# Hybrid shortconv–SSD trunk, one core: the output projection's second quarter as seven block products, the scan split 20 + 12, the scan's norms in column groups

## The chip, the cores and the metric

One core of one Trainium2 chip runs the whole kernel in one launch. The metric is the device time in microseconds. The kernel before takes 2596.71 us (median of three runs, 2595.24 to 2597.68).

## The reference, cut to what matters

A layer of a hybrid encoder over 2048 positions of width 1024, in float32:

```python
h = rmsnorm(x, norm_mix_w)
u_b, u_c, u_h, z, xbc, dt_raw = split(h @ w_in)
y_a = u_b * causal_conv3(u_c * u_h)                      # 1024 columns
y_b = ssd_mixer(z, xbc, dt_raw, ...)                     # 1024 columns
x = x + concat([y_a, y_b]) @ w_out                       # 2048 x 1024
h = rmsnorm(x, norm_mlp_w)
x = x + square(relu(h @ w_up)) @ w_down
return rmsnorm(x, final_norm_w)
```

The SSD mixer runs a causal convolution and SiLU on `xbc`, then a chunked state-space scan over 16 heads in two groups, a skip term, a gate `silu(z)`, and an RMSNorm over each group's 512 columns with a gain:

```python
gated = (y * silu(z)).reshape(b, t, 2, 512)
gated = rmsnorm(gated, norm_w.reshape(2, 512))
```

The output projection therefore falls into quarters: half `i` of its input columns (0: the short convolution's y_a, 1: the scan's y_b) for half `h` of the positions (1024 each).

## The kernel before, in words

Everything lives transposed, with columns on the 128 partitions and positions along the free axis, in blocks of 512 positions (`b` = 0 to 3, `NB`); a half `h` is two such blocks. Each float32 operand of a large product is split into a rounded part `hi` (a ScalarE copy) and a rest `lo` (a VectorE subtraction), and a product is three 128x128 by 128x512 matmuls: hi·hi, hi·lo, lo·hi (`mm3`, lines 118 to 120, or the lines 315 to 317 inside `chain`).

**Seven block products.** A pair of output column tiles for one half of the positions is a 2x2 block product (two halves of the contraction, two position blocks). `Seven.chain` does it by seven block products instead of eight, in the order b11, t1, t2, b21, t3, b22, t4; one product is four tiles of the contraction, so 12 matmuls, and a pair is 84 matmuls where plain work needs 96. The activations have to stand as seven combinations per tile (three double tiles and one single, `places`), made once and spilled to DRAM as `..._d[h][k]`; the weights of a pair are combined on the way in (`combine`: four more VectorE additions on 512 columns, and four splits). The first product's sum is copied by ScalarE into the bank of the fourth (line 322). After each product `chain` calls `evict`, takes split weights of the next pair (`ahead`), and calls `after(name)`: one step.

**Refresh.** A change of half needs new places: `fetch` (line 379) loads four double tiles at a time and `settle` (lines 390, 391) splits them, spread over the steps of the pair ahead by `refresh`.

**Order of the stages.** First half of the input projection (20 pairs, `PAIRS`); second half (22 pairs, `LATER`, with z-, x-, ch- and b-pairs); the output projection; then the MLP, which also goes by seven products. `Proj.pair` evicts each pair; for a b-pair (y_a) of half 0 it stores the seven combinations in `ym_d`, for half 1 the four plain blocks in `ys_d`.

**The output projection** (`Output`). Quarter (0, half 0) is four pairs by seven products (`Output.pair`, 28 steps). The other three quarters are plain: `Output.unit`, one output tile for one position block, 24 matmuls; units 16 to 31 are quarter (0, half 1), 32 to 47 quarter (1, half 0), 48 to 63 quarter (1, half 1). `fill` splits a plain input for them; `schedule` lists at which hook each input is loaded and split.

**The scan** (`Scan`) is 32 chunks (4 position blocks, 2 groups, 4 chunks of 128 positions), a generator that is advanced one stage at a time from the steps and hooks of the product work. Chunks 0 to 15 run beside the second half's pairs, one stage per step, with single buffers (`bufs` = 1, nine stages per chunk); what is left is drained when the last pair but one begins. Chunks 16 to 31 run beside the output projection, double buffered, eight stages per chunk. In a chunk, `front` transposes the inputs (`ptx`, line 1417), copies them (`xtok`, 1422), multiplies them by decays (1432), splits (1438, 1440) and prepares the decay matrix `dec` (1437, 1439, 1445); `back` does the state matmuls (`st`, lines 118 to 120), the off-diagonal (`yo`, 1459) and diagonal products (`yd`, 1462), updates the state and gates the result. After the fourth chunk of a group, the square sums of its 512 columns go through `Rstd.parts` (hi and lo of a 128x512 tile) and `Rstd.whole` (two 128x512 matmuls with ones, lines 186 and 187, a square root and a 512-wide reciprocal, 188 and 189); for half 0 the result is stored (`rn_d`) and loaded again by `norm`, for half 1 it stays.

PSUM has eight banks: three turn for the products x and y (`mm`), one for w (`mw`), one each for `yo` and `yd`, and two for small things (`tp`). SyncE issues nearly all transfers, in one queue. The order of instructions on each engine is that of the program, as far as the planner of the tile framework does not pass one that is not ready.

Of the kernel before, what the change touches and what calls it, by code (L numbers as in the profile page):

```python
# [16 lines left out]
P = 128  # L17
# [23 lines left out]
def trunk(ctx: ExitStack, tc: tile.TileContext, x, w_in, w_dt, w_out, w_up, w_down, cvec, hrow, out):  # L41
# [19 lines left out]
    ym_d = [dram.tile([P, 7, TB], F32, name=f"ym_d{k}") for k in range(4)]  # L61
    wide = lambda n, k: [dram.tile([P, k, TH], F32, name=f"{n}_d{h}") for h in range(2)]
    xs_d, sz_d, ys_d, yn_d = wide("xs", 12), wide("sz", 8), wide("ys", 8), wide("yn", 8)
    rn_d = dram.tile([P, NBB, G, TB], F32, name="rn_d")
# [151 lines left out]
    class Seven:  # L216
# [156 lines left out]
        def fetch(self, h, i):  # L373
# [91 lines left out]
        def refresh(self, name):  # L465
# [5 lines left out]
            if i is not None:  # L471
                self.got = self.fetch(1, i)

    class Proj(Seven):
# [5 lines left out]
        LATER = "z0 x0 z4 ch0 ch4 b0 x8 ch1 ch5 b1 x2 ch2 ch6 b2 x4 x10 ch3 ch7 b3 x6 z6 z2".split()  # L480
# [296 lines left out]
        def pair(self, h, what, ws, ahead, after):  # L777
# [31 lines left out]
            def evict(name, gi, pm):  # L809
# [19 lines left out]
                elif name == "b22":  # L829
# [4 lines left out]
                    elif kind == "b":  # L834
                        mul(to["c12"], to["c12"], self.cc[n][:, hi])
                        if h:
                            nc.sync.dma_start(ys_d[h][:, n], a)
                        else:
                            e = s["e"] = self.wide("et")
                            self.sub(e[:, 0], a[:, hi], a[:, lo])  # L840
                            self.sub(e[:, 1], b[:, hi], e[:, 0])
                            self.sub(a[:, hi], b[:, hi], a[:, hi])
                            nc.sync.dma_start(ym_d[n][:, 0:5:4], a.rearrange("p (a t) -> p a t", a=2))
                            nc.sync.dma_start(ym_d[n][:, 1:3], e)
# [7 lines left out]
                elif kind == "b":  # L852
                    mul(to["c21"], pm["x"], self.cc[n + 4][:, lo])
                    if h:
                        nc.sync.dma_start(ys_d[h][:, n + 4], b)
                    else:
                        nc.sync.dma_start(ym_d[n][:, 3:6:2], b.rearrange("p (a t) -> p a t", a=2))
                        t4 = self.tmp("t4")
                        self.sub(t4, b[:, lo], s["e"][:, 1])
                        nc.sync.dma_start(ym_d[n][:, 6], t4)  # L860
# [49 lines left out]
        def second_half(self, ws, side, stack):  # L910

            self.dt_open()
            dts = itertools.chain(*(self.dt_part(NBB + bb) for bb in range(NBB)))
            for m, what in enumerate(self.LATER):
                last = m + 1 == len(self.LATER)
                if m + 2 == len(self.LATER):
# [5 lines left out]
                    self.stored = (None, ym_d)  # L922
# [7 lines left out]
                def after(name):  # L930
                    if m or name == "t4":
                        next(dts, None)
                    next(side, None)
                    if m + 2 == len(self.LATER) and name == "t3":
                        self.got = self.fetch(1, 0)
                    if last:
                        if name == "t1":
                            next(ahead)
                        if name != "b11":
                            self.refresh(name)  # L940
# [402 lines left out]
    class Scan:  # L1343
# [104 lines left out]
        def back(self, n):  # L1448
# [35 lines left out]
            if c == 0:  # L1484
                self.ssq = self.sum_tile(b, g)
            ssq = self.ssq
            nc.vector.tensor_tensor(out=ssq[:, c * L : (c + 1) * L], in0=q4[:, 0], in1=q4[:, 1], op=ALU.add)
            if c == NC - 1:
                st = Rstd(None, self.part_tile, 512, TB)
                st.parts(ssq)  # L1490
            yield
            if c == NC - 1:
                if (b, g) == (NBB, 0):
                    ssq = uh.tile([P, TB], F32, tag="uh3", name="ssq", bufs=4)
                st.whole(ssq, "mw" if h else "tp")
                if h:
                    self.rn[b, g] = ssq
                else:
                    nc.sync.dma_start(rn_d[:, b, g], ssq)
# [5 lines left out]
        def sum_tile(self, b, g):  # L1505
            if b < NBB or (b, g) == (NBB, 0):
                return self.tile([TB], "ssq", 1)
            return uh.tile([P, TB], F32, tag="uh3", name="ssq", bufs=4)

        def part_tile(self, name):  # L1510
            if self.bufs == 1:
                return proj.e(name, TB)
# [374 lines left out]
```

## Time and profile before

| what | value |
| --- | --- |
| median of the runs | 2596.71 us |
| the profiled execution, its own time | 2599.74 us |
| its span in the trace | 2598.0 us |
| granted TensorE clock | 0.999 |
| PE, DVE, ACT busy | 99%, 75%, 54% |
| DMA | 546.4 MB, 62.4% of 16 engines' span |
| second half's pairs in the trace | 459.0 to 945.3 us |
| four output pairs | 945.3 to 1041.6 us |
| units 16 to 31, 32 to 47, 48 to 63 | from 1041.6, 1153.7 and 1263.0 us, to about 1351 us |

The stage times are read from the first matmul of each pair or unit. A PE record's length (0.39 us for a 128x512 matmul) is its way through the array; the spacing of the starts is what a matmul costs when the array is kept full. A row of a window gives the instructions that begin in it as "(x...)". In a timeline row, the bracket at the end is the idle time of that engine before the row and who ended it.

### The profile page before, as it was taken

The numbers are of one execution on the slowest core, as the hardware profiler recorded it, in microseconds if no ns is written. First come the engines' busy times: TensorE is split into PE (matmuls) and PEld (weight loads), VectorE is DVE, ScalarE is ACT, GpSimd is POOL, SyncE is SP. The second block draws the span as 40 slices with busy tenths as digits, with TensorE's granted clock in tenths as the row PEclk, the third lists the DMA queues.
The fourth block names the chain that finished last, engine by engine and source line by source line (L and its number), as shares of the span: only waits on it lengthen the run. The fifth ranks groups of instructions, "written<-read, shape, count | busy, mean of one in ns | idle before, by whom it ended". The sixth has DMA issues, their size and how long they took to land.

```text
span 2598.0 us, 33641 instructions
## 1 busy us (share of the span) xinstructions
PE 2572.3 (99%) x12027; PEld 2120.2 (82%) x12027; DVE 1937.1 (75%) x2627; ACT 1407.0 (54%) x2147; POOL 79.2 (3%) x99
## 2 busy tenths in 40 slices
PE   9999999999999999999999999999999999999998
PEld 7788878788888878888888888888887888888887
DVE  8877777867778688889877765644448887888885
ACT  6554345876567566656336555755556444444433
POOL 2110010000000000000000000000000000000001
PEclk9999999999999999999999999999999999999999
DMA  4555665755555478997656885855557655665762
GB/s 175 175 191 188 218 238 184 238 171 174 178 168 176 158 251 281 291 294 243 201 186 231 300 313 219 291 196 212 183 201 252 187 175 154 219 207 179 238 203 78
DMA packets 256345, 546.40 MB, mean 210 GB/s; under 512 B 26673, under 2 KB 93873, under 8 KB 256177
## 3 DMA queue, kind: packets, MB, share of 16 engines
q1 hardware_dynamic: 255600, 543.34, 62.4%
q8 instruction: 94, 1.54, 0.2%
q10 hardware_dynamic: 576, 0.92, 0.1%
q14 instruction: 75, 0.61, 0.1%
HBM read 359.87 MB, written 184.29 MB: 209 GB/s over the span
## 4 chain that ended last, share of the span: by engine, by line
PE 88%; DVE 5%; DMA 3%; issue 2%; ACT 2%; POOL 0%; SPq 0%; POOLq 0%; DVEq 0%; ACTq 0%
PE px L315 14%; PE px L317 14%; PE px L316 14%; PE py L315 7%; PE py L316 7%; PE py L317 7%; PE pm L118 4%; PE pm L119 4%; PE pm L120 4%; PE pw L315 3%; PE pw L317 3%; PE pw L316 3%; PE yd L1462 1%; DVE ul L391 1%; PE yo L1459 1%
## 5 line engine op out<-in xcount | busy, mean ns | idle before, releaser
L315 PE MATMUL px<-uh,whi 128*128 128x512 f32 x1736 | 679.6, 392 | 7.7 <-DVE acc L1176 3.3
L317 PE MATMUL px<-uh,wlo 128*128 128x512 f32 x1736 | 676.2, 390 | 0.5 <-DVE wlo L104 0.5
L316 PE MATMUL px<-ul,whi 128*128 128x512 f32 x1736 | 675.8, 389 | 0.0
L315 PEld LDWEIGHTS px<-uh,whi 128*128 128x128 f32 x1736 | 325.9, 188 | 82.2 <-DVE acc L1176 4.1
L317 PEld LDWEIGHTS px<-uh,wlo 128*128 128x128 f32 x1736 | 325.9, 188 | 70.9 <-issue 1.8
L316 PEld LDWEIGHTS px<-ul,whi 128*128 128x128 f32 x1736 | 326.0, 188 | 66.3
L104 DVE TENSOR_TENSOR wlo<-wraw,whi 128x512 fp32r<-128x512 f32 (+1 forms) x213 | 219.0, 1029 | 197.4 <-ACT whi L103 196.4
L103 ACT CAST whi<-s 128x1024 fp32r<-128x1024 f32 x218 | 228.3, 1047 | 216.6 <-PE py L316 97.7
L315 PE MATMUL py<-uh,whi 128*128 128x512 f32 x868 | 339.2, 391 | 2.3 <-ACT eb L850 1.5
L103 ACT CAST whi<-wraw 128x1024 fp32r<-128x1024 f32 x214 | 192.2, 899 | 274.5 <-PE px L316 214.1
L317 PE MATMUL py<-uh,wlo 128*128 128x512 f32 x868 | 338.0, 389 | 0.0
L316 PE MATMUL py<-ul,whi 128*128 128x512 f32 x868 | 338.0, 389 | 0.0
L104 DVE TENSOR_TENSOR wlo<-s,whi 128x1024 fp32r<-128x1024 f32 x218 | 265.1, 1216 | 76.2 <-ACT whi L103 75.2
L118 PE MATMUL pm<-uh,whi 128*128 128x512 f32 (+1 forms) x520 | 200.1, 385 | 0.8 <-ACT z L601 0.7
L119 PE MATMUL pm<-ul,whi 128*128 128x512 f32 (+1 forms) x520 | 197.8, 381 | 0.5 <-DVE ul L231 0.5
L120 PE MATMUL pm<-uh,wlo 128*128 128x512 f32 (+1 forms) x520 | 197.5, 380 | 0.0
L315 PEld LDWEIGHTS py<-uh,whi 128*128 128x128 f32 x868 | 163.0, 188 | 38.6 <-ACT eb L850 1.9
L316 PEld LDWEIGHTS py<-ul,whi 128*128 128x128 f32 x868 | 163.0, 188 | 34.2 <-issue 0.8
L317 PEld LDWEIGHTS py<-uh,wlo 128*128 128x128 f32 x868 | 163.0, 188 | 33.8
L315 PE MATMUL pw<-uh,whi 128*128 128x512 f32 x434 | 169.3, 390 | 0.0
L316 PE MATMUL pw<-ul,whi 128*128 128x512 f32 x434 | 168.9, 389 | 0.0
L317 PE MATMUL pw<-uh,wlo 128*128 128x512 f32 x434 | 168.9, 389 | 0.0
(265 smaller groups left out, 3613.1 us busy)
## 6 DMA issues: line engine op xcount, KB each, us to landing
hid_d<-e SPq DMA_DIRECT2D x96, 512.0 KB, 3.6
rh<-hid_d SPq DMA_DIRECT2D x96, 512.0 KB, 4.3
wraw<-w_in SPq DMA_DIRECT2D x68, 512.0 KB, 4.0
wraw<-w_down SPq DMA_DIRECT2D x104, 256.0 KB, 3.6
wraw<-w_up SPq DMA_DIRECT2D x48, 512.0 KB, 4.6
dec<-rd_d SPq DMA_DIRECT2D x32, 512.0 KB, 5.4
wraw<-w_out SPq DMA_DIRECT2D x32, 512.0 KB, 5.6
sums_d<-s SPq DMA_DIRECT2D x32, 512.0 KB, 4.4
```

Of the source, the lines that this page charges most:

```text
L103: nc.scalar.copy(hi, raw)
L104: split["last"] = eng.tensor_tensor(out=lo, in0=raw, in1=hi.bitcast(F32), op=ALU.subtract)
L118: nc.tensor.matmul(out, whi, hi, start=(k == 0), stop=False)
L119: nc.tensor.matmul(out, whi, lo, start=False, stop=False)
L120: nc.tensor.matmul(out, wlo, hi, start=False, stop=(k == nk - 1))
L315: nc.tensor.matmul(p, hi, h[0], start=not seeded and k == 0, stop=False, **kw)
L316: nc.tensor.matmul(p, hi, h[1], start=False, stop=False, **kw)
L317: nc.tensor.matmul(p, lo, h[0], start=False, stop=(k == len(g) - 1), **kw)
L391: nc.vector.tensor_tensor(out=p[i][1], in0=t, in1=p[i][0].bitcast(F32), op=ALU.subtract)
L1459: nc.tensor.matmul(yo[:, j * L : (j + 1) * L], state[:, j * P : (j + 1) * P], cT, start=True, stop=True)
L1462: nc.tensor.matmul(yd[(i % 2) * 64 : (i % 2) * 64 + 64, (i // 2) * L : (i // 2 + 1) * L], byhead(t["xdt"])[:, i, :], t["dec"][:, i % 2 * 4 ...
```

## The change

1. Quarter (0, half 1) also goes by seven products: `Output.pair` runs eight pairs (56 steps) instead of four, and units 16 to 31 are gone. The b-pairs of half 1 store seven combinations, as those of half 0 did. In the fourth output pair the places are refreshed from half 1 (`fetch`, `settle`), and `w_out[0]`'s combined weights are made a second time.
2. The scan runs 20 chunks beside the second half's pairs (four stages in three steps) and 12 beside the output projection (three stages in two steps, fewer around the refresh), now single buffered throughout. `LATER` is reordered so that chunks 16 to 19 find their inputs.
3. A group's norm: four matmuls that each take 32 columns of ones and 128 positions into 32 partitions of one PSUM tile, side by side, then a square root and a reciprocal on 128x128, stored as 128x128 and loaded again by a broadcast, for both halves. The split of the square sums is gone. The loaded norms of the first half's blocks take a buffer of the combined weights' pool (`us`, two buffers).
4. `fill` splits double tiles (128x1024) instead of single ones; the scaling by norm and gain has become a step of its own (`scale`). Units 32 to 47 are staggered as 48 to 63 were.

The diff, cut to its core:

```diff
-        LATER = "z0 x0 z4 ch0 ch4 b0 x8 ch1 ch5 b1 x2 ch2 ch6 b2 x4 x10 ch3 ch7 b3 x6 z6 z2".split()
+        LATER = "z0 x0 z4 ch0 ch4 b0 x8 ch1 ch5 b1 x2 ch2 x10 ch6 z2 b2 x4 ch3 ch7 b3 x6 z6".split()
...
                     elif kind == "b":
                         mul(to["c12"], to["c12"], self.cc[n][:, hi])
-                        if h:
-                            nc.sync.dma_start(ys_d[h][:, n], a)
-                        else:
-                            e = s["e"] = self.wide("et")
...
+                        e = s["e"] = self.wide("et")
+                        self.sub(e[:, 0], a[:, hi], a[:, lo])
+                        self.sub(e[:, 1], b[:, hi], e[:, 0])
+                        self.sub(a[:, hi], b[:, hi], a[:, hi])
+                        nc.sync.dma_start(ym_d[h][n][:, 0:5:4], a.rearrange("p (a t) -> p a t", a=2))
+                        nc.sync.dma_start(ym_d[h][n][:, 1:3], e)
...
-                    next(side, None)
+                    for _ in range(1 + (next(count) % 3 == 2)):
+                        next(side, None)
...
+            yield
             if c == NC - 1:
-                st = Rstd(None, self.part_tile, 512, TB)
-                st.parts(ssq)
-            yield
-            if c == NC - 1:
...
-                st.whole(ssq, "mw" if h else "tp")
...
+                pn = psum("tp", "pn", 2)
+                for i in range(NC):
+                    nc.tensor.matmul(
+                        pn[i * 32 : i * 32 + 32, 0:L], ones[:, 0:32], ssq[:, i * L : (i + 1) * L], start=True, stop=True
+                    )
+                r = ssq[:, 0:L]
+                nc.scalar.activation(r, pn[:, 0:L], AF.Sqrt, bias=eps, scale=1.0 / 512)
+                nc.vector.reciprocal(out=r, in_=r)
+                nc.sync.dma_start(rn_d[b][g], r)
...
+                if b < NBB:
+                    if g == 0:
+                        self.both = proj.sumtile("rn")
+                    t = self.both[:, g * TB : (g + 1) * TB]
...
-        UNITS = [None] * 16 + [(0, b, d) for d in range(KD) for b in ((2, 3) if d else (3, 2))]
...
+        UNITS = [None] * 32
+        UNITS += [(1, h + b, d - b) for h in (0, 2) for d in range(KD + 1) for b in (0, 1) if 0 <= d - b < KD]
...
         def pair(self, p, hook):
-            last = p == 3
+            last = p == 7
+            if p == 3:
+                proj.new = [{} for _ in range(4)]
+                sums_d["o4"] = "none"
...
+                if p == 2 and name == "t4":
+                    proj.got = proj.fetch(0)
+                if p == 3:
+                    if name == "t1":
+                        next(ahead)
+                    if name != "b11":
+                        proj.refresh(name)
                 hook(7 * p + n)
...
-            put(0, 3, 0, 20, (22, 23, 23, 24))
-            put(0, 2, 2, 25, (26, 27, 32, 32))
-            put(1, 0, 1, 32, (38, 40, 42, 44))
-            put(1, 1, 2, 58, (62, 62, 63, 63))
-            put(1, 2, 0, 68, (72, 74, 76, 78))
+            put(1, 0, 1, 46, (52, 53, 53, 54), (49, 49, 50, 50))
+            put(1, 1, 2, 54, (64, 65, 66, 66))
+            put(1, 2, 0, 70, (74, 76, 78, 80))
             put(1, 3, 1, 93, (96, 97, 98, 99))
...
-            side = scan.run(0, len(CHUNKS) // 2)
+            side = scan.run(0, 20)
...
-            scan.open(c2, "sp2", 2)
-            side = scan.run(len(CHUNKS) // 2, len(CHUNKS))
+            os = c2.enter_context(tc.tile_pool(name="os", bufs=1, reuse_waits="tile"))
+            proj.sumtile = lambda name: os.tile([P, 1024], F32, tag="us", name=name, bufs=2)
+            scan.open(c2, "sp2", 1)
+            side = scan.run(20, len(CHUNKS))
+            due = [0.0]
 
             def hook(at):
-                for _ in range(1 + at % 2 + (at % 8 == 4)):
+                due[0] += 0.5 if 21 <= at < 32 else 1.5
+                while due[0] >= 1:
+                    due[0] -= 1
                     next(side, None)
...
-            for p in range(4):
-                proj_out.pair(p, early)
-            for n in range(16, 48):
+            for p in range(8):
+                proj_out.pair(p, hook)
+            for n in range(32, 48):
                 proj_out.unit(n, hook)
```

More of the change, by code (lines that the diff above doesn't have):

```diff
@@ L1565, in run @@
                 yield
-                next(before, None)
+                next(back)
+                self.load(n + 1)
+                self.load_rows(n + 1)
                 yield
                 next(back)
-                self.load(n + 2)
-                self.load_rows(n + 1)
+                yield
                 yield
                 next(front, None)
-                yield
-                if next(before, "end") != "end":
-                    self.load_gate(n + 1)
                 yield
@@ L1580, in run @@
                 yield
+                next(back)
+                self.load_gate(n + 1)
+                yield
                 next(front, None)
                 yield
[L1583 to L1585 removed]
     class Output:
[L1592 to L1595 removed]
+        UNITS = [None] * 32
+        UNITS += [(1, h + b, d - b) for h in (0, 2) for d in range(KD + 1) for b in (0, 1) if 0 <= d - b < KD]
         TILES = {"c22": (1, 1, "xt"), "c12": (1, 0, "xt"), "c11": (0, 0, "facc"), "c21": (0, 1, "facc")}
@@ L1706, in unit @@
             whi, wlo = self.ws[m]
-            for k in range(KD):
-                if k == KD // 2:
+            for j in range(KD):
+                if j == KD // 2:
                     hook(2 * n)
-                mm3(pm, whi[:, k, :], wlo[:, k, :], *self.y[i, b][k], k, KD)
+                k = j // 2 + j % 2 * 4
+                mm3(pm, whi[:, k, :], wlo[:, k, :], *self.y[i, b][k], j, KD)
             t = self.xt.pop(n)
@@ L1731, in schedule, with put @@
             held = {}
-            def put(i, b, c, load, splits):
+            def put(i, b, c, load, splits, scales=None):
                 def fetch():
-                    held[i, b] = [self.fetch(i, b, k, self.raw) for k in range(0, KD, 2)]
-                    if i and b < NBB:
-                        for g in range(G):
-                            scan.norm(b, g)
+                    held[i, b] = [self.fetch(i, b, k, self.raw) for k in range(4)]
+                    for g in range(G):
+                        scan.norm(b, g)
                 self.todo.setdefault(load, []).append(fetch)
+                for j, at in enumerate(scales or splits):
+                    self.todo.setdefault(at, []).append(lambda j=j: self.scale(b, j, held[i, b][j]))
                 for j, at in enumerate(splits):
-                    self.todo.setdefault(at, []).append(lambda j=j: self.fill(i, b, c, 2 * j, held[i, b][j]))
-            put(0, 3, 0, 20, (22, 23, 23, 24))
-            put(0, 2, 2, 25, (26, 27, 32, 32))
-            put(1, 0, 1, 32, (38, 40, 42, 44))
-            put(1, 1, 2, 58, (62, 62, 63, 63))
-            put(1, 2, 0, 68, (72, 74, 76, 78))
+                    self.todo.setdefault(at, []).append(lambda j=j: self.fill(i, b, c, j, held[i, b][j]))
+            put(1, 0, 1, 46, (52, 53, 53, 54), (49, 49, 50, 50))
+            put(1, 1, 2, 54, (64, 65, 66, 66))
+            put(1, 2, 0, 70, (74, 76, 78, 80))
             put(1, 3, 1, 93, (96, 97, 98, 99))
@@ L1779, in hook @@
                     f()
-            def early(at):
-                for _ in range(1 + (at % 7 == 3)):
-                    next(side, None)
-                for f in proj_out.todo.pop(at, ()):
-                    f()
-            for p in range(4):
-                proj_out.pair(p, early)
-            for n in range(16, 48):
+            for p in range(8):
+                proj_out.pair(p, hook)
+            for n in range(32, 48):
                 proj_out.unit(n, hook)
```

147 lines of the change are left out of this document (46 added, 101 removed).

## The prediction

> **What bounds the kernel now.** I read the page's first lines, then a table by stage, then who TensorE (PE) waited for.
>
> ```profile
> span 2598.0 us, 33641 instructions
> PE 2572.3 (99%) x12027; PEld 2120.2 (82%) x12027; DVE 1937.1 (75%) x2627; ACT 1407.0 (54%) x2147; POOL 79.2 (3%) x99
> ```
>
> PE is the bound: what shortens PE's list shortens the time, unless a wait takes its place. The table (second half's pairs, output pairs, units 16 to 31, 32 to 47, 48 to 63, and 100 us of the MLP):
>
> ```profile
> 459.00:945.30 486.30, 482.23 (x2416) 398.79 (x2415) 362.04 (x503) 322.75 (x549) 21.73 (x40) 1.00 0.56 181
> 945.30:1041.60 96.30, 93.67 (x478) 75.55 (x478) 81.86 (x122) 61.13 (x121) 0.00 (x0) 1.00 0.90 289
> 1041.60:1153.70 112.10, 110.90 (x596) 91.31 (x595) 93.53 (x149) 69.81 (x146) 0.00 (x0) 1.00 0.92 290
> 1153.70:1263.00 109.30, 109.30 (x587) 90.69 (x586) 93.50 (x146) 64.97 (x131) 0.00 (x0) 1.00 0.74 235
> 1263.00:1351.00 88.00, 88.00 (x390) 72.88 (x389) 72.78 (x90) 28.64 (x33) 0.00 (x0) 1.00 0.62 201
> 1750.00:1850.00 100.00, 100.00 (x442) 82.79 (x442) 46.05 (x57) 54.03 (x81) 0.00 (x0) 1.00 0.54 191
> ```
>
> The columns are length, then busy time of PE, PEld, DVE, ACT, POOL, the clock, the DMA share and GB/s. The last row prices a matmul: 442 of 128x512 in 100 us, 0.226 us each. In the five stages touched PE idles only 7.9 us (892.0 less 884.1), the most that removing waits can give. DVE runs at 74% in the second half and 83 to 86% in the next three stages, DMA at 0.9 in two of them: little slack. PE's waits from 440 to 1351 us, largest four:
>
> ```profile
> PE st L118 <- ACT xtok L1438: 1.9, 2, 1.2
> PE px L315 <- DVE xt L1669: 1.6, 2, 1.0
> PE py L315 <- ACT eb L850: 1.5, 1, 1.5
> PE px L315 <- ACT pw L322: 1.3, 3, 0.9
> ```
>
> Two kinds: the scan's state matmul waits for its input, and a product waits for a bank that an eviction behind a refresh frees late.
>
> **Term 1, the products.** Units 16 to 31 held 16 x 24 = 384 matmuls; four pairs hold 4 x 84 = 336. 48 fewer x 0.226 = -10.8 us, all on PE.
>
> **Term 2, the norms.** Two ones-matmuls per group go, at 0.226 us each once PE is full, eight times 0.45. Four of 32 columns come. The nearest row is the step-size product `pd`, which puts four 32-column groups side by side, on 512 positions:
>
> ```profile
> 257.81 0.39 PE L317 MATMUL py<-uh,wlo 128*128 128x512 f32 x1
> 258.13 1.07 PE L667 MATMUL pd<-nb,rdt 128*32 128x512 f32 x8
> 259.13 0.50 PE L315 MATMUL py<-uh,whi 128*128 128x512 f32 x1
> 259.46 0.39 PE L316 MATMUL py<-ul,whi 128*128 128x512 f32 x1
> L189 DVE RECIPROCAL ssq<-ssq 128x512 f32<-128x512 f32 x8 | 26.8, 3350 | 4.7 <-ACT ssq L188 4.7
> L716 DVE RECIPROCAL dts<-dts 128x64 f32<-128x64 f32 x2 | 1.1, 548 | 0.0
> ```
>
> From 257.81 to 259.46 are 1.65 us, of which two ordinary matmuls are 0.45: the group costs 1.20, of which 1.00 is between the starts and 0.20 beside them. With a quarter of the positions, 0.25 + 0.20 = 0.45 (an estimate): the same as now. Lower bound 0.22 each (-1.8 in all), upper bound the whole 1.20 (+6.0). I take 0, because a 128-position group must stream less than a 512-position one. *Rule:* the Trainium skill, TensorEngine Tiling (Array Packing), Key Properties, says that changing the tiling mode drains TensorE. The 0.20 us beside the group agrees with a small drain; no row has 128 positions. If the drain were all of the 1.20 us, the sum below would lose 6.0.
>
> Off PE the norm gets cheaper: a reciprocal took 3.35 us on 512 columns and 0.55 on 64, so about 0.95 on 128. DVE, whose burst of 3.35 us held up what stands behind it, gains 2.4 us eight times, and the `lo` subtraction (0.69) goes too. On SP's queue the store of the norm waits for the shorter chain.
>
> **Term 3, 20 chunks in the second half.** DVE there gains and loses:
>
> ```profile
> L1432 DVE TENSOR_TENSOR stmp<-xtok,dd 128x512 f32<-128x512 f32 x62 | 41.5, 686 | 10.6 <-ACT xtok L1422 10.3
> L1487 DVE TENSOR_TENSOR ssq<-stmp 128x128 f32<-128x128 f32 x32 | 9.2, 288 | 0.5
> ```
>
> These are the first and last of the scan's 12 DVE groups, 8.0 us per chunk (five stages of 0.69 us and the first row's two, 1.22 for `dec`, four small ones). Four chunks add 32 us; the b-pairs' four subtractions of 0.69 us, four times, 11 us; shorter norms take back about 12. So 362 becomes some 393 us in a stage that grows by four chunks' matmuls (about 4 us each) to 502: 78% instead of 74%. DVE does not become the bound, but the beats come closer. How far ahead the scan's inputs are, in a usual chunk and in the worst after the start:
>
> ```profile
> 719.92 0.60 PE L1417 MATMUL ptx<-ident,xd 128*128 128x128 f32 x4
> 725.62 0.68 DVE L1440 TENSOR_TENSOR stmp<-stmp,xtok 128x512 fp32r<-128x512 f32 x1
> 734.31 0.39 PE L118 MATMUL st<-xtok,btok 128*128 128x512 f32 x1
> 804.75 0.60 PE L1417 MATMUL ptx<-ident,xd 128*128 128x128 f32 x4
> 815.65 0.63 DVE L1440 TENSOR_TENSOR stmp<-stmp,xtok 128x512 fp32r<-128x512 f32 x1
> 819.62 0.39 PE L118 MATMUL st<-xtok,btok 128*128 128x512 f32 x1
> ```
>
> From the transposes to the state matmul are 14.4 us, five stages, one per step of 12 x 0.226 = 2.7 us. At four stages in three steps, five stages are four steps in three chunks of four, and three in the fourth: 11.7 or 9.0 us. The split's end lies 6.4 us after the transposes in the usual chunk (slack 8.0, then 2.6 at the least) and 11.5 in the worst (slack 3.3, then none, and up to 2.5 us short). If the five chunks with the short distance miss it by 0.4 us on the mean, that is 2. I take +2, nearer to the usual chunk's row, of which there are more; bounds 0 (the worst chunk stands right behind a 3.35 us reciprocal, which goes) and +20 (all like the worst and somewhat later, as the queues fill: five x 2.5 and fifteen x 0.5). Waiting at `st` on PE's queue are then the main products themselves.
>
> **Term 4, the refresh in the fourth output pair.** New: 28 blocks of 256 KB fetched, and 16 splits. What the same step cost at the change of half:
>
> ```profile
> 457.60 0.50 PE L315 MATMUL px<-uh,whi 128*128 128x512 f32 x1 [0.83 <-DVE eb L807]
> 459.57 1.05 ACT L390 CAST uh<-rb 128x1024 fp32r<-128x1024 f32 x1 [1.36 <-DMA rb<-hm_d]
> 463.04 0.59 ACT L850 ACTIVATE eb<-px 128x512 f32<-128x512 f32 x1
> 463.68 0.50 PE L315 MATMUL py<-uh,whi 128*128 128x512 f32 x1 [1.48 <-ACT eb L850]
> 926.20:945.30 19.10, 19.10 (x86) 15.79 (x85) 14.98 (x18) 13.90 (x18) 0.00 (x0) 1.00 0.88 318
> 945.30:966.50 21.20, 19.63 (x85) 15.62 (x85) 16.16 (x19) 11.52 (x16) 0.00 (x0) 1.00 0.93 318
> ```
>
> ACT waits for the landing, evictions queue behind it, PE waits for the bank: 1.48 us there, and 0.83 before it, where a subtraction of the splits stood ahead of the eviction on DVE. At the other refresh, ahead of the output pairs, PE idles 1.6 us in the pair after. In an output pair the evictions are DVE's, but ACT still copies the first product (L322), and the splits are behind the landings on both. The same pattern, so +2.6: above both rows, since scan transfers now run beside it. Bounds +0.5 and +13: 7.3 MB of fetches with 4 MB of weights, residuals, stores and half a chunk's transfers, at 318 GB/s, take 36 us, where the eight steps last some 23.
>
> **Term 5, the buffer of `us`.** The rows of a combined weight's split, of an addition for it and of the scaling by norm and gain:
>
> ```profile
> L104 DVE TENSOR_TENSOR wlo<-s,whi 128x1024 fp32r<-128x1024 f32 x49 | 59.8, 1219 | 18.5 <-ACT whi L103 18.1
> L234 DVE TENSOR_TENSOR s<-s,wraw 128x512 f32<-128x512 f32 x5 | 3.4, 687 | 0.0
> L1619 DVE SCALAR_TENSOR_TENSOR ry<-ry,cv,rn 128x512 f32<-128x512 f32 x16 | 11.4, 747 | 1.9 <-DMA rn<-rn_d 1.9
> ```
>
> The loaded norms take one of two buffers in the seventh pair, between that pair's s12 and s34. s34 needs s12, so it must wait until the four `scale` steps (eight DVE operations of 0.75 us) have let the norms go, at hooks 49 and 50, and its split is wanted by the eighth pair's fifth product, hook 53: three steps, 8 us, for two subtractions (1.4), a copy (1.05) and a subtraction (1.22), on a DVE that also has block (1, 0) to split. Behind s34 on DVE and ACT are r1's split and the next evictions. I take +1.5; bounds 0 (these 3.7 us fit into 8) and +6 (the eight scales before them).
>
>
> **Term 6, what goes.** Units 16 to 31 had one wait, where half 1's plain inputs were split beside the scan. And the burst of drained chunk stages before the first output pair kept SP's queue 10.6 us behind one norm, with DMA at 0.26 of its time, and then everything at once:
>
> ```profile
> 1071.95 0.49 PE L118 MATMUL st<-xtok,btok 128*128 128x512 f32 x1 [1.20 <-ACT xtok L1438]
> SPq L1499 <- DVE ssq L189: 10.6, 1, 10.6
> 906.30:926.20 19.90, 19.90 (x93) 15.99 (x90) 17.08 (x20) 12.38 (x16) 0.00 (x0) 1.00 0.26 94
> ```
>
> 20 chunks have 184 stages (four and nine each); 140 steps call 186. So no burst is left, the first loads come earlier, and I take 1.2 and, of the 1.6 us, all: -2.8 (bounds 0 and -4).
>
> Edits that cost nothing: `fill` on double tiles and the units' new order (as many matmuls, the same splits); the pairs' extra splits, additions and two more evictions each, some 6 us of DVE per pair (four additions of 0.69, 2 us of splits, two evictions of 0.69) beside 84 x 0.226 = 19 us of products. That last cover is thin, in the eighth pair above all; its failure is in term 5's upper end. Single buffers beside the output projection: a chunk then takes nine stages, six steps of 2.7 us and its own matmuls, some 20 us, and the `dec` transfer that must fit between two chunks lands in 5.4 us:
>
> ```profile
> dec<-rd_d SPq DMA_DIRECT2D x32, 512.0 KB, 5.4
> ```
>
> **Sum:** -10.8 + 0 + 2.0 + 2.6 + 1.5 - 2.8 = -7.5 us on the span of 2598.0. The profiled execution took 2599.74, 3.0 over the median of 2596.71; the same difference from the median gives 2589.2.
>
> **The rivals.** *All hidden:* terms 3 to 5 at nothing, since PE idled less than 8 us in all of this before: -10.8 - 2.8 = -13.6, 2583. Against it: every refresh in this trace cost PE something. *Eaten up:* the refresh waits for its bytes by half of the 13 us (6.5), the buffer of `us` costs 4, the chunks 2: -10.8 + 6.5 + 4 + 2 - 2.8 = -1.1, 2595.6. For it: DMA at 0.93 in 945 to 966 us. *The mode change at its full 1.20 us:* +6.0 on my sum, -1.5, 2595; against it, the 0.20 us beside the group. *Slower, the scan's beat:* each chunk's state matmul in the second half waits 1 us on the mean, because ACT and DVE lag as they do in the worst chunk; 20 us more, -10.8 - 2.8 + 4.1 + 20 = +10.5, 2607. It decides from 0.75 us per chunk on. For it: the 2.5 us short above. Against it: that chunk stood behind the norm's reciprocal, and beside units, three stages in 5.4 us of products went by with one wait.
>
> **How the numbers follow.** A measurement of this kernel tells about 0.2% (5.2 us) from no change. Likeliest, the sum, 2586 to 2593, a tenth of it above 2591.5: 0.37. All hidden: 0.21. Eaten up: 0.20. Mode change: 0.04. Slower: 0.18. Faster: 0.33 + 0.21 = 0.54; same 0.04 + 0.20 + 0.04 = 0.28; slower 0.18. The range takes in the hidden case and the lower part of the slow one: 2582 to 2604.
>
> **What would show it.** The second half's pairs end near 961 us, with no wait at `st` above 1 us; 48 fewer 128x512 matmuls from there to the MLP; the norm's four groups within 0.5 us; PE idle of 1 to 4 us in the fourth and fifth output pair, released by ACT or DVE behind a `rb`-like load; a wait for `wlo` or `whi` of s34 in the eighth pair. The prediction is wrong if PE's idle time from 459 to 1340 us exceeds some 15 us, or if the norms' groups stand over 1 us apart.

## The result, and the profile after

The changed kernel is slower: 2625.81 us in the median (2623.34 to 2628.55) against 2597.19 (2595.24 to 2601.29) for the kernel before, a ratio of 1.0108, 95% interval 1.0091 to 1.0126. That is 28.6 us lost where 7.5 were to be won. One run of e12 below, 2838.16 us at a granted clock of 0.849, is a slow one and stands in no ratio. First come two lines of the changed kernel's page, the span and the busy time:

```profile
span 2621.6 us, 33756 instructions
PE 2577.2 (98%) x12027; PEld 2115.4 (81%) x12027; DVE 1946.4 (74%) x2651; ACT 1408.8 (54%) x2135; POOL 77.1 (3%) x99
```

The table by stage (second half's pairs, the eight output pairs, units 32 to 47, units 48 to 63; columns as in the prediction), and its sum:

```profile
460.10:963.40 503.30, 500.67 (x2585) 409.43 (x2583) 387.10 (x568) 345.54 (x616) 19.81 (x40) 1.00 0.61 197
963.40:1162.30 198.90, 187.98 (x957) 151.40 (x957) 170.36 (x250) 116.83 (x216) 0.00 (x0) 0.99 0.84 264
1162.30:1286.90 124.60, 109.99 (x534) 88.69 (x533) 84.45 (x124) 55.86 (x102) 0.00 (x0) 0.92 0.71 221
1286.90:1374.90 88.00, 88.00 (x390) 72.88 (x389) 71.14 (x89) 30.46 (x34) 0.00 (x0) 1.00 0.66 218
sum 914.80, PE 886.64 PEld 722.39 DVE 713.05 ACT 548.69 POOL 19.81; mean PE 221.66 PEld 180.60 DVE 178.26 ACT 137.17 POOL 4.95
```

The stretch is 22.8 us longer than before (892.0), nearly the whole growth of the span (23.6). PE idles 28.2 us in it instead of 7.9: 2.6 in the second half, 10.9 in the output pairs, 14.6 in units 32 to 47, and none in the last stage. Its busy time is no smaller (886.6 against 884.1) although 48 products went, in part because the clock is granted at 0.92 in the third stage. (The page counts 12027 PE instructions in both kernels: 48 products fewer, and 48 records more for the norms, eight groups of 8 instead of 2.) So the second half, where the prediction put its slower case, is in order; the loss is in 320 us of output projection. Who PE waited for, 440 to 1375 us:

```profile
PE pn L1488 <- ACT xtok L1418: 10.2, 1, 10.2
PE st L118 <- ACT xtok L1434: 6.4, 6, 2.3
PE py L315 <- DVE facc L1627: 2.6, 1, 2.6
PE px L315 <- DVE xt L1627: 2.4, 2, 1.2
PE st L119 <- DVE stmp L1436: 2.4, 6, 0.6
```

One wait of 10.2 us, and many small ones. The large one is read from ACT's timeline and from the chain of waits, both at 1150 to 1179 us. ACT:

```profile
1160.01 0.62 ACT L1478 ACTIVATE stmp<-y 128x512 f32<-128x512 f32 x1
1169.41 0.40 ACT L1433 ACTIVATE dec<-dec,dd 128x128 f32<-128x128 f32 x1 [8.79 <-DMA dec<-rd_d]
1173.64 0.57 ACT L1418 COPY xtok<-ptx 128x512 f32<-128x512 f32 x1
```

The chain (start, length, what):

```profile
1153.21 11.94 DMA wraw<-w_out
1165.23 4.42 DMA ry<-yn_d
1169.72 1.02 ACT whi L103
...
1173.73 0.49 ACT xtok L1418
...
1174.27 0.65 PE pn L1488 x8
1174.92 0.73 PE pm L120
1175.65 0.43 PE pm L118
```

A weight load that took 11.94 us, another load behind it, and ACT, whose list is in order, 8.79 us at the decay matrix `dec`, which came late too; behind it stood the copy that frees the `tp` bank for the norm's matmuls `pn`. ACT's waits for `dec` from 945 us on, in the kernel before and in the changed one:

```profile
ACT dec L1437 <- DMA dec<-rd_d: 1.2, 1, 1.2
```

```profile
ACT dec L1433 <- DMA dec<-rd_d: 29.4, 10, 8.8
```

What stood ahead of the weight load were two loads of norms, by SyncE's row; and in the 8 us from 1152 on the DMA engines are 64% busy and move only 111 GB/s, where the output pairs as a whole had 264 at 84%:

```profile
1146.88 1.21 SPq L1511 DMA_DIRECT2D rn<-rn_d  x2
1152.00:1160.00 8.00, 7.98 (x48) 6.23 (x47) 8.00 (x12) 4.36 (x7) 0.00 (x0) 1.00 0.64 111
```

What is different about these loads, the DMA issues show, before and after (transfers, size, median us to landing):

```profile
rn<-rn_d SPq DMA_DIRECT2D x4, 256.0 KB, 7.2
```

```profile
rn<-rn_d SPq DMA_DIRECT2D x8, 256.0 KB, 9.4
DMA to landing us min/median/max: 7.7/9.4/14.9
```

There are twice as many, each slower. In the kernel before, each partition loads a row of 2 KB of its own. The changed kernel stores 128 x 128 values and loads them by a broadcast: every one of 128 partitions reads the same four rows of 512 bytes, 16 KB apart. Neither short pieces nor a common row need be slow by themselves. In the same kernel `xd` is also one transfer of 256 KB in 512-byte pieces, each from a place of its own, and in `dec` all 128 partitions read the same 4 KB:

```profile
xd<-xs_d SPq DMA_DIRECT2D x32, 256.0 KB, 3.7
dec<-rd_d SPq DMA_DIRECT2D x32, 512.0 KB, 5.2
```

### The profile page after: what moved, and what is told of

It is laid out like the page before. It is cut to its first block, busy times and chain, and to the rows that moved or that the text cites. A ratio compares the mean times of both kernels' runs of the same rounds, so it can differ in the third digit from the quotient of the medians.

```text
span 2621.6 us, 33756 instructions
## 1 busy us (share of the span) xinstructions
PE 2577.2 (98%) x12027; PEld 2115.4 (81%) x12027; DVE 1946.4 (74%) x2651; ACT 1408.8 (54%) x2135; POOL 77.1 (3%) x99
## 4 chain that ended last, share of the span: by engine, by line
PE 77%; DMA 7%; DVE 7%; ACT 5%; issue 3%; SPq 0%; POOL 0%; POOLq 0%; DVEq 0%; ACTq 0%
PE px L315 13%; PE px L317 13%; PE px L316 13%; PE py L315 6%; PE py L316 6%; PE py L317 6%; PE pw L315 3%; PE pw L317 3%; PE pw L316 3%; DMA dec<-rd_d 3%; PE pm L118 2%; PE pm L120 2%; PE pm L119 2%; ACT dec L1433 1%; DVE wlo L104 1%
## 5 line engine op out<-in xcount | busy, mean ns | idle before, releaser
L315 PE MATMUL px<-uh,whi 128*128 128x512 f32 x1800 | 705.8, 392 | 7.9 <-DVE xt L1627 2.4
L317 PE MATMUL px<-uh,wlo 128*128 128x512 f32 x1800 | 701.3, 390 | 0.0
L316 PE MATMUL px<-ul,whi 128*128 128x512 f32 x1800 | 701.0, 389 | 0.0
L315 PE MATMUL py<-uh,whi 128*128 128x512 f32 x900 | 353.0, 392 | 3.1 <-DVE facc L1627 2.6
L317 PE MATMUL py<-uh,wlo 128*128 128x512 f32 x900 | 351.4, 390 | 0.0
L316 PE MATMUL py<-ul,whi 128*128 128x512 f32 x900 | 351.3, 390 | 0.0
L103 ACT CAST whi<-wraw 128x1024 fp32r<-128x1024 f32 (+1 forms) x214 | 190.5, 890 | 278.0 <-PE px L316 224.1
L391 DVE TENSOR_TENSOR ul<-rh,uh 128x1024 fp32r<-128x1024 f32 (+1 forms) x128 | 138.7, 1087 | 33.1 <-ACT uh L390 32.9
L390 ACT CAST uh<-rh 128x1024 fp32r<-128x1024 f32 (+1 forms) x128 | 120.3, 943 | 74.6 <-PE py L317 60.5
L118 PE MATMUL pm<-uh,whi 128*128 128x512 f32 (+1 forms) x392 | 150.2, 384 | 0.7 <-ACT z L601 0.7
```

The costliest lines, as they stand in the source:

```text
L103: nc.scalar.copy(hi, raw)
L118: nc.tensor.matmul(out, whi, hi, start=(k == 0), stop=False)
L315: nc.tensor.matmul(p, hi, h[0], start=not seeded and k == 0, stop=False, **kw)
L316: nc.tensor.matmul(p, hi, h[1], start=False, stop=False, **kw)
L317: nc.tensor.matmul(p, lo, h[0], start=False, stop=(k == len(g) - 1), **kw)
L390: nc.scalar.copy(p[i][0], t)
```

## The experiments

The theories behind the first four: the single-buffered scan beside the output, whose `dec` is on time only if it lands in 5 us (A); the refresh (B); the norms' buffer among the combined weights, and the packed splits (C); the norm's matmuls and the bank that they wait for (D).

**e1, the kernel before with the scan beside the output single buffered, nine stages per chunk.**

```diff
-            scan.open(c2, "sp2", 2)
+            scan.open(c2, "sp2", 1)
...
-                for _ in range(1 + at % 2 + (at % 8 == 4)):
+                for _ in range(1 + at % 2 + (at % 4 == 0)):
...
-                for _ in range(1 + (at % 7 == 3)):
+                for _ in range(1 + (at % 7 in (3, 5))):
```

> The kernel before with one thing of the change alone: the scan beside the output projection single buffered (nine stages per chunk, called often enough for 16 chunks), still plain units in the second quarter and the old norms. Theory A (the one buffer of the decay matrix: its load can only start after the chunk before has used it, and ScalarE, in order, stands at it): 15 to 40 us slower than before, and ScalarE's waits for the decay load grow from 1.2 us to over 20 us. Theory B (the second quarter's refresh and its transfers cost the time) and theory C (the norms' buffer in the pool of combined weights and the packed splits): within 5 us of before, decay waits under 5 us.

Measured: 2609.59 us, ratio 1.0044 (1.0029 to 1.0059), some 12 us slower. ACT's waits for `dec`:

```profile
ACT dec L1438 <- DMA dec<-rd_d: 21.2, 11, 7.0
```

The cover that the prediction took for granted is not there, but 12 us is less than theory A asked (15 to 40) and less than the whole. The one buffer is loaded again right behind the diagonal products of the chunk before, and in 12 of the 16 chunks ACT is free for its first operation on `dec` less than 5.9 us after that load's issue, which is the median time to landing. One chunk, SyncE's row and two of ACT's:

```profile
1151.37 0.38 SPq L1387 DMA_DIRECT2D dec<-rd_d  x1
1154.37 0.63 ACT L1483 ACTIVATE stmp<-y 128x512 f32<-128x512 f32 x1
1157.54 1.57 ACT L1438 ACTIVATE dec<-dec,dd 128x128 f32<-128x128 f32 x5 [2.55 <-DMA dec<-rd_d]
```

**e2, the changed kernel without the loads of `dec` for chunks 20 to 31** (`xd`, a tile of the same chunk that is loaded in any case, stands in).

```diff
-            nc.sync.dma_start(t["dec"], rd_d[b][0, r0 : r0 + HG].partition_broadcast(P))
+            t["src"] = self.bufs == 1 and n >= 20
+            if not t["src"]:
+                nc.sync.dma_start(t["dec"], ...)
...
-                    nc.scalar.activation(dec[:, i], dec[:, i], ...)
+                    nc.scalar.activation(dec[:, i], t["xd"][:, i % 4] if t["src"] else dec[:, i], ...)
```

> The changed kernel without the loads of the decay matrix of chunks 20 to 31 (the first operation reads another tile of the same shape in their place, so the values are others; the instructions are the same). Theory A: 20 to 32 us of the 28 come back, to 2594 to 2606 us, and the single wait of 10 us at the norm's matmuls goes. Theory B: the DMA has 6 MB less to move beside the output, so 2 to 8 us come back, and the fourth pair's waits stay. Theory C: no change by more than 4 us, the 10 us wait at the norm stays.

Measured: 2608.76, ratio 1.0049 (1.0032 to 1.0065): 17 us back, less than the theory wanted. PE's wait at `pn` is 0.2 us here, but ACT now stands 16.9 us at the same line for `xd`, another load that comes late. The run takes away one victim of a clog and 6 MB of traffic; it doesn't say what clogs.

**e3, the changed kernel without the refresh:** half 0's blocks are multiplied again.

```diff
-                if p == 2 and name == "t4":
-                    proj.got = proj.fetch(0)
...
-                    if name != "b11":
-                        proj.refresh(name)
...
-                proj.places = proj.new
```

> The changed kernel without the fetch and split of the new places in the fourth output pair (pairs four to seven read the old places; their transfers and splits are left out). Theory A: under 6 us faster than the changed kernel, since the decay waits are in later pairs and units; about 2620 to 2626 us. Theory B: 15 to 30 us faster, 2596 to 2610 us. Theory C: under 3 us faster.

Measured: 2621.05, ratio 1.0095 (1.0076 to 1.0113): 4.8 us less, with intervals that overlap.

**e4, the kernel before with only the norms in column groups,** stored and loaded as in the change.

```diff
-                st = Rstd(None, self.part_tile, 512, TB)
-                st.parts(ssq)
...
+                pn = psum("tp", "pn", 2)
+                for i in range(NC): ...
+                nc.sync.dma_start(rn_d[b][g], r)
...
-                nc.sync.dma_start(t, rn_d[:, b, g])
+                row = rn_d[b][g].rearrange("(q p) l -> p q l", p=32)[0]
+                nc.sync.dma_start(t.rearrange("p (q l) -> p q l", q=NC), row.partition_broadcast(P))
```

> The kernel before with the norms in column groups alone (four 32-column matmuls on 128 positions, a 128-wide root and reciprocal, stored and loaded again by a broadcast for both halves). Every theory that puts the loss elsewhere: between 3 us faster and 1 us slower than before, a norm's group within 0.5 us on TensorE. Theory D (changing the array's mode, and waiting for the norm's bank, costs the time): 8 us or more slower.

Measured: 2618.58, ratio 1.0078 (1.0063 to 1.0093): 21 us by the norms alone, where every theory but D had 1 us at most. But the time is not where D put it: a norm's group of matmuls takes some 0.36 us on TensorE, from its start to that of the next matmul. Three windows of this kernel: while the transfers ahead of two norm loads land (these are issued at 1045.70), while the norms come, and after:

```profile
1046.00:1052.00 6.00, 6.00 (x40) 5.08 (x41) 1.22 (x2) 3.48 (x6) 0.00 (x0) 1.00 0.99 346
1053.50:1060.00 6.50, 6.50 (x33) 5.42 (x33) 2.64 (x5) 2.14 (x6) 0.00 (x0) 1.00 0.84 64
1062.00:1068.00 6.00, 2.73 (x13) 1.92 (x11) 0.87 (x1) 1.32 (x2) 0.00 (x0) 0.96 0.98 348
```

The last two columns are the reading: in the second window the 16 DMA engines are 84% busy and move 64 GB/s, a fifth of what they moved just before. That is 6.5 x 0.84 x 16 = 87 us of engine time for 0.42 MB. The trace's DMA packets say what took it: 584 packets of 512 bytes that begin in this window took 142 ns each on the mean, 83 us in all, while those of the window before and the window after took 31 and 28. What was to land then lands late, and in the third window PE idles 3.3 of 6 us. DVE waits for the norm itself, and PE for the scan's inputs behind it on DVE and ACT; a row of DVE's timeline and two of PE's waits in this kernel:

```profile
1057.82 0.75 DVE L1619 SCALAR_TENSOR_TENSOR ry<-ry,cv,rn 128x512 f32<-128x512 f32 x1 [3.86 <-DMA rn<-rn_d]
```

```profile
PE st L119 <- DVE stmp L1440: 9.7, 4, 6.5
PE st L118 <- ACT xtok L1438: 6.6, 3, 5.8
```

Now the norm load had to be told from the norm's matmuls, and the common address from the short pieces.

**e5, the changed kernel, but 32 partitions read 32 different (equal) rows,** in four loads of the same 512-byte pieces.

```diff
-                row = rn_d[b][g].rearrange("(q p) l -> p q l", p=32)[0]
-                nc.sync.dma_start(t.rearrange("p (q l) -> p q l", q=NC), row.partition_broadcast(P))
+                rows = rn_d[b][g].rearrange("(q p) l -> p q l", p=32)
+                for j in range(4):
+                    nc.sync.dma_start(t[32 * j : 32 * j + 32].rearrange("p (q l) -> p q l", q=NC), rows)
```

> The changed kernel; the load of a norm takes as many 512-byte pieces, but each 32 partitions read 32 equal rows in DRAM (64 KB) instead of all 128 partitions reading one and the same row (four loads for one). Theory E (128 partitions reading the same four addresses hold the DMA engines: in the kernel with the norms alone 6.5 us at 0.84 busy moved 64 GB/s): the norm's load lands in 4 to 7 us instead of 9.4, the 10 us wait of TensorE at the norm goes, and 8 to 18 us of the 28 come back, to 2608 to 2618 us. Theory F (it is the number of short pieces, wherever they lie): no change beyond 4 us. Theory A (single buffers alone): no change beyond 4 us.

Measured: 2604.45, ratio 1.0024 (1.0014 to 1.0033): 21.4 us back, a little more than theory E said. ACT's waits for `dec` fall from 29.4 to 11.4 us, PE's wait at `pn` from 10.2 to 1.6 and its idle time in the stages from 28.2 to 17.0. The loads:

```profile
rn<-rn_d SPq DMA_DIRECT2D x32, 64.0 KB, 4.5
```

**e6, the changed kernel, stored so that all 128 partitions read one row of 2 KB.** Same common address, one piece instead of four.

```diff
-                nc.sync.dma_start(rn_d[b][g], r)
+                for i in range(NC):
+                    nc.sync.dma_start(rn_d[b][g][:, i * L : (i + 1) * L], r[32 * i : 32 * i + 32])
...
+                nc.sync.dma_start(t, rn_d[b][g][0].partition_broadcast(P))
```

> The changed kernel; the norm stands in DRAM as one row of 2 KB (four stores of 32 partitions), and all 128 partitions read this same row, in one piece of 2 KB each. Theory E: the same addresses are still read 128 times, so the load stays slow (over 8 us) and at most 6 us come back. Theory F: a quarter of the pieces, 8 to 18 us come back. If the row is held only because four pieces lie far apart in it, as with F.

Measured: 2607.34, ratio 1.0033 (1.0023 to 1.0044): 18.5 us back. So theory E as it stood, the common address alone, is out too; it is the common rows in short pieces. (e6 also makes one row of four that lay 16 KB apart, so the length of the pieces and their distance are not told apart.)

```profile
rn<-rn_d SPq DMA_DIRECT2D x8, 256.0 KB, 6.7
```

**e7, e4 with 32 rows of 2 KB,** each read by four partitions in four loads (the store is e6's).

```diff
-                row = rn_d[b][g].rearrange("(q p) l -> p q l", p=32)[0]
-                nc.sync.dma_start(t.rearrange("p (q l) -> p q l", q=NC), row.partition_broadcast(P))
+                for j in range(4):
+                    nc.sync.dma_start(t[32 * j : 32 * j + 32], rn_d[b][g])
```

> The kernel before with the norms in column groups alone, stored as 32 rows of 2 KB and loaded with each 32 partitions reading 32 different rows, 2 KB each. Theories E and F: the 21 us of the norms alone go, between 4 us faster and 4 us slower than before. Theory D (array mode, bank): still 8 us or more slower.

Measured: 2596.21, ratio 0.9994 (0.9984 to 1.0003). The norms in column groups cost nothing by themselves; all of e4's 21 us was the load, and theory D is out. The window that was clogged, in this kernel, where norms are on the way, too (eight loads are issued from 1049.92 to 1057.94):

```profile
1053.50:1060.00 6.50, 6.50 (x51) 5.27 (x48) 5.25 (x9) 3.53 (x10) 0.00 (x0) 1.00 0.81 258
```

The same share, four times the bytes, though the other transfers in the two windows are not the same ones. Some 7 us of e5 against the kernel before remained.

**e8, the changed kernel with ACT's work on `dec` ordered behind the same chunk's copies out of PSUM.**

```diff
-            self.act = nc.scalar.copy(hi, pb[:, 0:P])
+            self.act = t["own"] = nc.scalar.copy(hi, pb[:, 0:P])
...
-            with tc.issue_after(self.cast.ins) if self.cast else nullcontext():
+            with tc.issue_after(t["own"].ins):
```

> The changed kernel; ScalarE's first operations on the decay matrix of a chunk are put behind that chunk's own copies from PSUM (they stood behind the chunk before's rounding), in both parts of the scan. Theory A (ScalarE, in order, stands at the late decay load, and TensorE's small banks wait behind): the 10 us wait at the norm goes and 8 to 20 us come back, 2606 to 2618 us. Theory E: the loads are as late as before and the state matmuls wait instead; within 6 us of the changed kernel, faster or slower.

Measured: 2619.27, ratio 1.0077 (1.0062 to 1.0092): 6.5 us back, between the bounds of the two theories. PE's wait at `pn` falls from 10.2 to 2.4 us, and its waits for the scan's inputs and for `facc` grow: the order on ACT passes the lateness on to PE, but most of it gets there by other ways.

**e9, e5 with `dec` in two halves over three buffers, loaded ahead.**

```diff
-            t["dec"] = self.tile([HG, L], "dec")
...
+            d.append(self.tile([4, L], "dec", 3 if self.begin else 2))
+            nc.sync.dma_start(d[-1], rd_d[b][0, r0 : r0 + 4].partition_broadcast(P))
...
```

> The changed kernel with e5's norm load, and beside the output the decay matrix as two halves in three buffers: the next chunk's inputs and first half are loaded ahead of the state matmuls of the chunk before, the second half right behind them. Theory A (what is left above the products' 10.8 us is the single buffer): ScalarE's waits for the decay load fall from 11.4 us to under 5 us, and 5 to 12 us come off e5, to 2592 to 2600 us. Rival (it is the packed refresh and transfers in general): within 4 us of e5's 2604.5 us, and other waits take the place.

Measured: 2603.71, ratio 1.0029 (1.0019 to 1.0039): nothing gained on e5. But the edit did not do what it was made for: ACT's waits for `dec` did not fall from e5's 11.4 us, they grew.

```profile
ACT dec L1443 <- DMA dec<-rd_d: 18.8, 9, 5.0
```

So the run doesn't tell what `dec` on time would be worth.

**e10, e5 with the scan's loads one stage earlier.**

```diff
                 next(back)
+                self.load(n + 1)
                 yield
                 next(back)
-                self.load(n + 1)
                 self.load_rows(n + 1)
```

> The changed kernel with e5's norm load; a chunk's loads are issued one stage earlier, right behind the state matmuls of the chunk before (both parts of the scan). Theory A: 2 to 6 us off e5's 2604.5 us. Rival: within 2 us of e5.

Measured: 2602.05, ratio 1.0014 (1.0004 to 1.0023), 2.4 us under e5, with overlapping intervals.

**e11, e5 without the refresh,** which is left out by e3's diff.

> The changed kernel with e5's norm load and without fetch and split of the new places in the fourth output pair (pairs four to seven read the old ones). This prices term 4 of the prediction without the norm load beside it: by the prediction 2.6 us off e5's 2604.5 us; if the refresh is the main part of what is left, 8 us or more.

Measured: 2596.79, ratio 0.9995 (0.9985 to 1.0004): the refresh costs 7.7 us there.

**e12, e5 with 24 chunks beside the second half's pairs and 8 beside the output** (`LATER` reordered for it).

```diff
-                    for _ in range(1 + (next(count) % 3 == 2)):
+                    for _ in range(1 + (next(count) % 7 in (1, 3, 5, 6))):
...
-            side = scan.run(0, 20)
+            side = scan.run(0, 24)
...
-            side = scan.run(20, len(CHUNKS))
+            side = scan.run(24, len(CHUNKS))
...
-                due[0] += 0.5 if 21 <= at < 32 else 1.5
+                due[0] += 0.5 if 21 <= at < 32 else 1.05
```

> The changed kernel with e5's norm load, and 24 chunks beside the second half's pairs (11 stages in 7 steps; the x- and z-pairs earlier in the order) and 8 beside the output (about one stage per step). If what is left is the density of the scan beside the output: 8 to 15 us off e5, 2590 to 2597 us, the second half growing by four chunks' matmuls (15 us) and no more. If the second half is full at 20 chunks: its stage grows by over 22 us, and the sum stays within 5 us of e5 or is slower.

Measured: 2597.80, ratio 0.9996 (0.9986 to 1.0005): 6.7 us less than e5, a little under the 8 of the first theory. The second half's pairs end at 983 us and take 17 us more than e5's, so by the second theory's own sign (22) that stage was not full at 20 chunks.

**e13, e12 and e10's diff together: all the computation. e14, e13 without the refresh** (e3's diff).

> The changed kernel with the norm load's rows spread, 24 chunks beside the second half's pairs and 8 beside the output, and the scan's loads one stage earlier; nothing is left out. Theory A (what is left over the kernel before is the dense single-buffered scan and the refresh, and their costs add): 2597.8 by the split alone, less the 2.4 us that the earlier loads saved with 12 chunks beside the output, or a little less of it since only 8 are left: about 2596, so ratio 0.999. Theory B (earlier loads only helped where 12 chunks were crowded): 2597.8, no change from the split alone.

> The same kernel without the refresh in the fourth output pair: half 1's input blocks are neither fetched nor split, so the second four output pairs multiply half 0's blocks again (the output's second half is not the reference's); as many products are issued. Theory A (the 48 products that went are worth their 10.8 us of TensorE's time, and only waits hide it): refresh back 7.7 us, so 2587 to 2590, ratio about 0.996. Theory B (TensorE's time saved by the products is given back by something else, such as a lower clock or the beat of the other engines in the pairs): it stays at 2593 to 2598.

Measured: e13 2597.47, ratio 0.9999 (0.9990 to 1.0008); e14 2598.14, ratio 1.0000 (0.9991 to 1.0009). The prices do not add, against the theory that sent e14: the refresh that cost 7.7 us beside 12 chunks costs nothing beside 8 that these intervals show. So with everything mended the 10.8 us still do not appear. Where they go, the sums of the table by stage tell (459 us to the end of unit 63, in each kernel's own times): e7, which has the same norms and 48 more products, e5, and e13.

```profile
sum 891.50, PE 884.30 PEld 726.70 DVE 680.49 ACT 541.19 POOL 18.66; mean PE 176.86 PEld 145.34 DVE 136.10 ACT 108.24 POOL 3.73
```

```profile
sum 897.00, PE 880.02 PEld 716.60 DVE 712.32 ACT 548.51 POOL 19.49; mean PE 220.00 PEld 179.15 DVE 178.08 ACT 137.13 POOL 4.87
```

```profile
sum 891.00, PE 877.49 PEld 715.31 DVE 713.64 ACT 555.90 POOL 27.99; mean PE 219.37 PEld 178.83 DVE 178.41 ACT 138.98 POOL 7.00
```

From e7 to e13 PE's busy time falls by 6.8 us and its idle time grows from 7.2 to 13.5, of which 8.3 are in the second half's pairs (3.2 in e7): nothing is left. DVE has 33 us more to do in the same time. No version that was run beats the kernel before by more than a measurement tells.

## Why the prediction was wrong

It said 2589.2 in a range of 2582 to 2604; the time is outside it, on the side of the smaller chance, and the slower rival's reason (the scan's beat in the second half) was not the cause.

**The step that failed: the norm's load, which had no term.** Term 2 priced the matmuls, the reciprocal and the store; "loaded again by a broadcast" stood in the change and was costed at nothing, with eight loads instead of four and 512 pieces of 512 bytes each on the queue. It cost 21 of the 28.6 us (e4 puts them in, e5 and e7 take them out). The prediction's own rows had `rn` landing and DVE waiting for it ("1.9 <-DMA rn<-rn_d"), and DMA at 0.9 in two of the stages; a transfer whose form changes there should have had bounds.

**Also mis-sized: "single buffers beside the output projection" at nothing.** e1 measured 12 us with 16 chunks; e12, with four of the changed kernel's 12 chunks taken away, gave 6.7 back. The argument was that a chunk of some 20 us leaves room for a transfer that lands in 5.4. The landing was about right (5.9 in e1 and, beside the output, in the kernel before); the room was not. It is not the chunk but the time from the load's issue, right behind the last use of `dec` in one chunk, to ACT's first use in the next: 4.6 us in e1's median. How much of the loss is `dec`, and which of the other single buffers matters, stays open: e9, which was to bring `dec` in time, did not.

**Term 4, the refresh: 2.6 predicted; 4.8 in e3, 7.7 between e5 and e11, nothing between e13 and e14.** The first two lie within the bounds given (0.5 to 13), the last under them. It is not a number of its own: it changed with the number of chunks beside it.

**Term 1, the products: -10.8 predicted; -6.8 (e13) or -4.3 (e5) of PE's busy time came.** The count was right: the page of e7 has 12075 PE instructions and that of e13 12027, which is 48 fewer. The other 4 us of busy time are mostly waits too short to be seen as idle. Products start every 0.226 us but a record is 0.39 us long, so a pause of less than 0.16 us between two of them counts as busy. In the stretch of the sums above, the scan's and the norms' records take as long in e13 as in e7 (115.6 and 115.5 us, from each start to the next, less idle time). But 132 products of e13 and 102 of e7 stand over 0.30 us ahead of the next start, and that is 3.4 us more. The clock is no cause here: it reads 1.00 in every stage of both kernels. So nearly all that the products save comes back as waiting, 6.3 us idle and 3.4 in short pauses. The largest single wait that the trace names in e13 comes to less than 3 us in total, and no run singles one out: what TensorE waits for in place of the products stays open.

**Right.** Term 2 on PE: the group takes some 0.36 us in e7, where 0.45 was estimated (0.65 in the chain above and 0.42 in e11's, below, both behind a wait), and PE's busy time with the column groups (e7, 884.3) is that of before (884.1), so the mode-change rival is out. The rule quoted there, from the Trainium skill, TensorEngine Tiling (Array Packing), Key Properties, has a drain at such a change and gives it no figure; these numbers leave room for a small one only. The reciprocal took 0.95 us as estimated:

```profile
L1493 DVE RECIPROCAL ssq<-ssq x8: 942/947/954, 559.9 to 1266.3; 128x128 f32<-128x128 f32 x8
```

Term 3: the second half's pairs grew by 17.0 us for four chunks, where 16 of matmuls and 2 of waits were said, and end at 963.4 (961 said); the waits did not come, though, since PE's idle time there fell from 4.1 to 2.6 us. Term 6: SyncE's wait behind the norm went from 10.6 to 1.6 us; what that gave PE was not told apart. Term 5 was not measured alone: DVE waited 11.9 us for the norms to land in the changed kernel and 2.6 in e5, and what the `us` buffer cost was not told apart from that. The prediction's own alarm, PE idle above some 15 us from 459 to 1340, rang at 28.2.

## What to carry to other kernels

When a change rewrites a store and the load that answers it, price the load by its pieces: how many, how long, and how many of them read the same bytes. A load can cost more through the transfers that it holds up than through those who wait for it. And where an edit takes work from an engine that is 99% busy by giving each helper (DVE, the queue, the buffers) a little more, the prices measured one at a time do not add; price the helpers' slack in the stage, not the edit.

## What was not expected of the hardware

**Short pieces of a common row.** In e4's middle window 87 us of DMA engine time moved 0.42 MB, in e7's 84 us (6.5 x 0.81 x 16) moved 1.68 MB. Spreading the rows (e5) or making one long piece of them (e6) each cured it; why short pieces of common rows are slow was not found. The Trainium skill, DMA: Bandwidth & Descriptors, Specifications, gives 512 bytes as the least transfer for line rate; these pieces are 512 bytes and, all from the same rows, far from it.

**The clock after a wait.** After the wait of 10.2 us PE's matmuls came every 0.43 us (the chain's row at 1175.65) instead of 0.226, and a window there has a granted clock of 0.57:

```profile
1175.00:1179.00 4.00, 4.00 (x11) 3.14 (x12) 3.71 (x6) 2.49 (x4) 0.00 (x0) 0.57 0.38 124
```

In e11 a wait of only 2.5 us was enough; one of the same length in e12 (2.5 us, PE at `px` for ACT's `pw`) was followed by products every 0.23 us. PE's wait in e11, and the chain behind it:

```profile
PE pn L1488 <- ACT xtok L1418: 2.5, 1, 2.5
```

```profile
1158.97 0.42 PE pn L1488 x8
1159.39 0.43 PE pm L120
...
1162.77 0.43 PE pm L119
1163.20 0.26 PE pm L120
1163.46 0.23 PE pm L118
```

Nine matmuls at about 0.2 us too much are 1.8 us on top of the wait. The Trainium skill, TensorE: Matmul & The Clock Gate, Part 1, has the half rate follow an idle window of about 3.4 us that runs freely, and last about as long; the half rate and the 4 us of recovery agree, and the wait that sufficed in e11 was shorter.
